# Linear attention in slots: the gates cut behind the scan, and values and scores used one slot later

## The chip, the cores and the metric

The kernel runs on one core of a Trainium2 chip. The core has a matrix engine (TensorE, PE in the profile; its weight loads are listed apart as PEld), a vector engine (VectorE, DVE), a scalar engine (ScalarE, ACT), and a queue that issues transfers (SyncE, SP); a further engine, GpSimd (POOL), does almost nothing here. Matrix products are written to PSUM, which is held in banks; all other tiles lie in SBUF. The metric is the time of one execution on the device in microseconds (us). The times shown are the median and the extremes of three runs; the profile is of one execution more, whose own time stands beside it.

## The reference

One encoder block on a sequence of 1024 positions and 1024 features, in float32. What is computed in the part that the change touches is gated linear attention in two directions, with four heads, keys of 128 and values of 256 features:

```
z   = code @ up + bias                      # per direction, 16 -> 512
lg  = max(log_sigmoid(z) / 16, -0.5)
b   = cumsum(lg)        within a chunk
q'  = q * exp(b);  k' = k * exp(-b)
scores = where(mask, q' k'^T, 0)
o   = scores @ v + q' @ state
state = exp(b_last) * state + k_tail^T v
out = rms_norm(o_fwd + o_bwd) * silu(r)
```

The forward direction takes a position's own key in, the backward direction does not. Around it stand the input projection of the normalised input, a windowed attention with eight heads, the projections of both branches with their sigmoid gates, and a feed-forward block.

## The kernel before

The kernel is one unrolled program. Matrix products are of float32 values split in a high and a low part (`vh` and `vl`, `kth` and `ktl`, `sh` and `sl`, `wh` and `wl` for weights): ACT makes the high part by a copy, VectorE the low part by a subtraction, and `mm3` adds three products. All of them go through `mm`, so they bear the line L76. Products on unsplit float32 tiles (`th` with `q2f`, `thb` with `q2b`, `en` with `q2f` and `q2b`) go through the same line.

The stage of interest runs over four heads (`hd`) and eight chunks of 128 positions each (`c`), so 32 steps n = hd * 8 + c, in a software pipeline of slots. The table `at` says which function runs in which slot for which chunk:

- `g_gates` (L514) in slot n, for two chunks at once, so in even slots alone. It loads `qk`, does the matmul of `lrS` with `upS` (z), the exponential (L537), a minimum (L539), a logarithm (L540), the scan (L544) into `cs`, the chunk sums `sm`, three subtractions into `e` (L550 to L553), two exponentials over `cs` and `e` (L557, L558), and four products: two into `en` and two into `q2` (L560 to L564), of which the first is `q2f` and the second `q2b`. `e` and `cs` have one buffer each.
- `g_scores` (L566) in slot n + 2: it loads and splits the values (`vr`; `vh`, `vl`), transposes `en` on PE (L578) and splits the result (`kth`, `ktl`), makes the scores of both directions (`sc`), merges them with the mask `tri` into `sp` (L587, L588) and splits that (`sh` L591, `sl` L592).
- `g_out` (L594) in slot n + 3: the products of keys and values (`kv`), the running forward state `pf` (L608), its scaled copy `th` (L607), a copy `kb` for the backward state (L610), and the output `o` from `sh`, `sl`, `vh`, `vl`, `th` and `q2f`, copied to `ob` (L619).
- `g_back_out` (L633) in slot `cb`: the backward share from `thb` and `q2b`, then the next step of the backward state (`g_back`), and for even chunks the normalisation of two chunks (L651).
- `g_turn` (L653) in slot `tt`: two transposes on PE, a copy (L659) and two transfers to DRAM scratch. Both chunks of a pair have the same `tt`.

Within a slot the functions run in the order gates, turns, backward output, output, scores, and `slot` spreads `n` filler matmuls between them. Fillers are the matmuls of the dense projections that later stages need (`dense`, `fill`); what is left over is done in the windowed attention behind. The order on PE is the program's own (`manual_schedule`). On the other engines a planner fixes the order when the program is built, by the order in which instructions are written and by when it thinks their inputs are ready; each engine then runs its list in that order.

PSUM tiles of this stage come from `chtile`, a ring of four banks (`ch`); the dense projections use four others (`mm`). SBUF tiles of the stage come from `gtile`, by tag, with two buffers where nothing else is said.

Of the kernel before, what the change touches and what calls it, by code (L numbers as in the profile page):

```python
# [9 lines left out]
FR = mybir.dt.float32r  # L10
# [4 lines left out]
P = 128  # L15
# [3 lines left out]
NH = 4  # L19
NC = 8  # L20
# [10 lines left out]
def body(tc, i, out):  # L31
    nc = tc.nc
    with ExitStack() as root:
# [8 lines left out]
        def nm(s):  # L42
            uid[0] += 1
            return f"{s}_{uid[0]}"
# [4 lines left out]
        def chtile(shape, dt=F32):  # L49
            return psc.tile(list(shape), dt, tag="ch", name=nm("ch"))  # L50
# [24 lines left out]
        def mm(o, a, b, start, stop):  # L75
            nc.tensor.matmul(o, a, b, start=start, stop=stop)  # L76
# [116 lines left out]
        def fill(n):  # L193

            while n > 0 and dense:
                try:
                    next(dense[0])
                    n -= 1
                except StopIteration:
                    dense.pop(0)  # L200

        def need(key):
            while key not in scr:
                fill(12)

        def slot(stages, n):

            stages = [f for f in stages if f] or [lambda: None]
            done = 0
            for j, f in enumerate(stages):  # L210
                f()
                t = n * (j + 1) // len(stages)
                fill(t - done)
                done = t
# [195 lines left out]
        with tc.manual_schedule(engines={mybir.EngineType.PE}):  # L410
# [8 lines left out]
            for k in range(KT):  # L419
# [5 lines left out]
                c = slice((k % 4) * P, (k % 4 + 1) * P)  # L425
# [17 lines left out]
            for f in range(0, NG, 2):  # L443
                x_first(f)
                if f == 0:
                    for s in range(2):
                        v = chtile((P, HT))
# [41 lines left out]
        for s in range(2):  # L489
            c = slice(s * HT, (s + 1) * HT)  # L490
# [18 lines left out]
        def gtile(tag, shape=(P, 256), dt=F32, bufs=2):  # L509
            return gt.tile(list(shape), dt, tag=tag, name=nm(tag), bufs=bufs)  # L510

        gla = {}

        def g_gates(hd, c):  # L514


            pr = Chunk()
            for j in range(2):
                a = gla[hd, c + j] = Chunk()
                a.pr, a.j, a.t = pr, j, slice(j * P, (j + 1) * P)  # L520
            s, co = c // 4, (c % 4) * P
            for nme in ("q", "k"):
                need((f"{nme}{hd}", s))
            qk = gtile("qk", (P, 2, 256))
            nc.sync.dma_start(out=qk[:, 0], in_=scr[f"q{hd}", s][:, co:co + 256])
            nc.sync.dma_start(out=qk[:, 1], in_=scr[f"k{hd}", s][:, co:co + 256])
            if hd == 0:

                r = rstd[:, c * P:(c + 2) * P]
                nc.vector.scalar_tensor_tensor(qk[:, 0], qk[:, 0], 128 ** -0.5, r, op0=ALU.mult, op1=ALU.mult)  # L530
                nc.vector.tensor_tensor(qk[:, 1], qk[:, 1], r, op=ALU.mult)
            z = chtile((P, 2, 256))
            for d in range(2):
                mm(z[:, d], upS[:, d, hd * P:(hd + 1) * P], lrS[:, c * P:(c + 2) * P], True, True)
            e = gtile("e", (P, 2, 2, P), bufs=1)
            ef = e.rearrange("p d j t -> p (d j t)")
            nc.scalar.activation(ef, z.rearrange("p d t -> p (d t)"), AF.Exp, scale=-1.0)  # L537

            nc.vector.tensor_scalar(ef, ef, float(np.expm1(8.0)), None, op0=ALU.min)  # L539
            nc.scalar.activation(ef, ef, AF.Ln, bias=ones[:, 0:1])  # L540

            cs = gtile("cs", (P, 2, 2, P), bufs=1)
            csf = cs.rearrange("p d j t -> p (d j t)")
            nc.vector.tensor_tensor_scan(csf, mask.rearrange("p c t -> p (c t)"), ef, 0.0, op0=ALU.mult, op1=ALU.add)  # L544

            pr.sm = gtile("sm", (P, 2, 2, 2), bufs=16)
            nc.vector.tensor_scalar(pr.sm, cs[:, :, :, 63:128:64], -1.0 / 16, None, op0=ALU.mult)
            nc.vector.tensor_tensor(pr.sm[:, :, :, 1], pr.sm[:, :, :, 1], pr.sm[:, :, :, 0], op=ALU.subtract)

            nc.vector.tensor_tensor(e[:, 0], cs[:, 0], cs[:, 0, :, 63:64].to_broadcast([P, 2, P]), op=ALU.subtract)  # L550
            nc.vector.tensor_tensor(e[:, 1, :, 1:P], cs[:, 1, :, 0:P - 1], cs[:, 1, :, 63:64].to_broadcast([P, 2, P - 1]),
                                    op=ALU.subtract)
            nc.vector.tensor_scalar(e[:, 1, :, 0:1], cs[:, 1, :, 63:64], -1.0, None, op0=ALU.mult)  # L553

            x1 = cs.rearrange("p d j t -> p d (j t)")
            x2 = e.rearrange("p d j t -> p d (j t)")
            nc.scalar.activation(csf, ef, AF.Exp, scale=-1.0 / 16)  # L557
            nc.scalar.activation(ef, ef, AF.Exp, scale=1.0 / 16)  # L558
            pr.en = gtile("en", (P, 2, 256))
            nc.vector.tensor_tensor(pr.en[:, 0], x2[:, 0], qk[:, 1], op=ALU.mult)  # L560
            nc.vector.tensor_tensor(pr.en[:, 1], x1[:, 1], qk[:, 1], op=ALU.mult)
            pr.q2 = (gtile("q2f"), gtile(f"q2b{c}", bufs=(3, 2, 2, 1)[c // 2]))
            nc.vector.tensor_tensor(pr.q2[0], x1[:, 0], qk[:, 0], op=ALU.mult)
            nc.vector.tensor_tensor(pr.q2[1], x2[:, 1], qk[:, 0], op=ALU.mult)  # L564

        def g_scores(hd, c):  # L566

            a = gla[hd, c]
            need((f"v{hd // 2}", c))
            vr = gtile("vr", bufs=1)  # L570
            nc.sync.dma_start(out=vr, in_=scr[f"v{hd // 2}", c][:, (hd % 2) * 256:(hd % 2) * 256 + 256])
            a.vh = gtile("vh", dt=FR)
            a.vl = gtile("vl", dt=FR)
            nc.scalar.activation(a.vh, vr, AF.Copy)
            nc.vector.tensor_tensor(a.vl, vr, a.vh.bitcast(F32), op=ALU.subtract)
            kt = chtile((P, 2, P))
            for d in range(2):
                nc.tensor.transpose(kt[:, d], a.pr.en[:, d, a.t], ident)  # L578
            a.kth = gtile("kth", (P, 2, P), FR)
            a.ktl = gtile("ktl", (P, 2, P), FR)  # L580
            nc.scalar.activation(a.kth, kt, AF.Copy)
            nc.vector.tensor_tensor(a.ktl, kt, a.kth.bitcast(F32), op=ALU.subtract)
            sc = chtile((P, 2, P))
            for d in range(2):
                mm(sc[:, d], a.pr.en[:, d, a.t], a.pr.q2[d][:, a.t], True, True)
            sp = gtile("sp", (P, P))
            nc.scalar.copy(sp, sc[:, 0])  # L587
            nc.vector.copy_predicated(sp, tri, sc[:, 1])  # L588
            a.sh = gtile("sh", (P, P), FR)
            a.sl = gtile("sl", (P, P), FR)  # L590
            nc.vector.tensor_copy(a.sh, sp)  # L591
            nc.vector.tensor_tensor(a.sl, sp, a.sh.bitcast(F32), op=ALU.subtract)  # L592

# [72 lines left out]
        at = {}  # L666
        last = 0
        for n in range(NH * NC):
            hd, c = divmod(n, NC)
            cb = hd * NC + NC + 3 + (NC - 1 - c)  # L670
            tt = cb + c % 2 + 2
            for j, (t, f) in enumerate(((n, g_gates), (n + 2, g_scores), (n + 3, g_out),
                                        (cb, g_back_out), (tt, g_turn))):
                if j or c % 2 == 0:
                    at[t, j + (j == 4 and c % 2)] = (f, hd, c)
                last = max(last, t)
        with tc.manual_schedule(engines={mybir.EngineType.PE}):
            fill(24)
            for t in range(last + 1):
                n = 46 if t < 3 else 20 if t < 6 else 15 if t < NH * NC + 3 else 12 if t < last - 1 else 18  # L680
                slot([(lambda v=at[t, j]: v[0](*v[1:])) if (t, j) in at else None for j in (0, 5, 4, 3, 2, 1)], n)
        glas.close()


# [202 lines left out]
        for n in range(2 * KT):  # L887
            g, t = divmod(n, KT)
# [522 lines left out]
```

## Time and profile before

| | us |
|---|---|
| median of three runs | 1656.65 |
| fastest and slowest run | 1655.84, 1657.62 |
| the profiled execution | 1657.74 |
| its span, first to last instruction | 1656.0 |
| PE busy in the span | 1640.2 |
| VectorE busy in the span | 1238.4 |
| ACT busy in the span | 878.7 |

The profile is a page about the one profiled execution, and a set of views of its trace: the busy time of each engine in a stretch of the span, groups of equal instructions (by line, engine, operation, and tile written <- tiles read), the waits (who stood idle until whose instruction ended), and the single instructions in order of time. Times in it count from the first instruction. Matmuls overlap each other, so the busy time of PE holds no idle time shorter than that overlap. An engine's wait is put down to the instruction that released it last.

### The profile page before, as it was taken

To read this page: it belongs to the slowest core of one execution; us is meant where nothing else is said; L and a number is where in the kernel's file an instruction comes from. 1 tells how busy PE (TensorE), PEld (TensorE's weight loads), DVE (VectorE), ACT (ScalarE), POOL (GpSimd) and SP (SyncE) were. 2 spreads that over 40 slices of the span, in tenths; PEclk is the share of its full clock that TensorE was granted. 3 is DMA by queue.
4 is the path that set the end of the run, shared out by engine and by line. 5 is a ranking of instruction groups with operands and counts; after the bars stand their busy time and mean duration, and the time that the engine had idled before them with its cause. 6 is when DMAs were issued, how large, how long until landed. Compare 5 with 4: busy or idle time off the path is not lost.

```text
span 1656.0 us, 23230 instructions
## 1 busy us (share of the span) xinstructions
PE 1640.2 (99%) x7636; PEld 1357.4 (82%) x7636; DVE 1238.4 (75%) x2548; ACT 878.7 (53%) x1847; POOL 0.2 (0%) x4
## 2 busy tenths in 40 slices
PE   9999999999999999999999999999999999999999
PEld 7888888788888888887888888888888888888887
DVE  8766676677864998756886579887777778779655
ACT  8522234688887587766555456433333333354442
POOL 0000000000000000000000000000000000000000
PEclk9999999999999999999999999999999999999999
DMA  7444336444435633327866645353234443496433
GB/s 234 140 140 146 117 99 194 122 124 137 137 116 162 202 103 108 96 77 251 260 211 188 180 141 162 108 178 109 90 110 152 158 140 134 163 346 197 146 97 120
DMA packets 157497, 252.38 MB, mean 152 GB/s; under 512 B 18142, under 2 KB 43486, under 8 KB 157376
## 3 DMA queue, kind: packets, MB, share of 16 engines
q1 hardware_dynamic: 157376, 250.90, 47.7%
q8 instruction: 60, 0.98, 0.2%
q14 instruction: 61, 0.50, 0.1%
HBM read 183.46 MB, written 67.37 MB: 151 GB/s over the span
## 4 chain that ended last, share of the span: by engine, by line
PE 86%; DVE 6%; ACT 5%; DMA 2%; issue 1%; SPq 0%; DVEq 0%; ACTq 0%
PE mm L76 28%; PE mm L306 9%; PE mm L308 9%; PE mm L307 9%; PE mm L1224 7%; PE ch L76 5%; PE ch L1224 5%; PE ch L308 4%; PE ch L306 4%; PE ch L307 4%; PE ch L847 1%; DVE cs L544 1%; DVE wl L72 1%; DMA kvr<-skv 1%; ACT wh L70 1%
## 5 line engine op out<-in xcount | busy, mean ns | idle before, releaser
L72 DVE TENSOR_TENSOR wl<-wr,wh 128x512 fp32r<-128x512 f32 x226 | 154.2, 685 | 52.0 <-ACT wh L70 48.6
L298 ACT ACTIVATE wh<-ws 128x512 fp32r<-128x512 f32 x132 | 83.3, 632 | 199.2 <-PE mm L307 103.8
L70 ACT ACTIVATE wh<-wr 128x512 fp32r<-128x512 f32 x226 | 140.5, 626 | 86.1 <-PE mm L76 59.1
L76 PE MATMUL mm<-wl,xh 128*128 128x512 f32 x320 | 131.4, 411 | 0.0
L76 PE MATMUL mm<-wh,xh 128*128 128x512 f32 x320 | 130.8, 409 | 0.0
L76 PE MATMUL mm<-wh,xl 128*128 128x512 f32 x320 | 130.5, 408 | 0.0
L299 DVE TENSOR_TENSOR wl<-ws,wh 128x512 fp32r<-128x512 f32 x132 | 90.3, 684 | 28.9 <-ACT wh L298 27.6
L298 ACT ACTIVATE wh<-wr 128x512 fp32r<-128x512 f32 x69 | 43.6, 632 | 123.7 <-issue 49.4
L298 ACT ACTIVATE wh<-a 128x512 fp32r<-128x512 f32 x64 | 40.5, 633 | 89.9 <-PE ch L1224 42.3
L299 DVE TENSOR_TENSOR wl<-a,wh 128x512 fp32r<-128x512 f32 x64 | 44.2, 690 | 41.9 <-ACT wh L298 41.3
L76 PEld LDWEIGHTS mm<-wh,xl 128*128 128x128 f32 x320 | 60.3, 188 | 10.4
L76 PEld LDWEIGHTS mm<-wl,xh 128*128 128x128 f32 x320 | 60.3, 189 | 9.9
L1224 PE MATMUL mm<-hh,wh 128*128 128x512 f32 x176 | 68.5, 389 | 0.0
L1224 PE MATMUL mm<-hl,wh 128*128 128x512 f32 x176 | 68.5, 389 | 0.0
L1224 PE MATMUL mm<-hh,wl 128*128 128x512 f32 x176 | 68.5, 389 | 0.0
L76 PEld LDWEIGHTS mm<-wh,xh 128*128 128x128 f32 x320 | 60.3, 188 | 9.9
L76 PE MATMUL mm<-xl,wh 128*128 128x512 f32 x160 | 65.6, 410 | 0.0
L76 PE MATMUL mm<-xh,wh 128*128 128x512 f32 x160 | 64.7, 405 | 0.1
L76 PE MATMUL mm<-xh,wl 128*128 128x512 f32 x160 | 57.7, 401 | 0.0
L1194 DVE TENSOR_TENSOR hl<-hr,hh 128x512 fp32r<-128x512 f32 x75 | 51.3, 684 | 4.8 <-ACT hh L1193 4.8
L1224 PE MATMUL ch<-hh,wh 128*128 128x512 f32 x132 | 51.3, 389 | 0.0
L1224 PE MATMUL ch<-hl,wh 128*128 128x512 f32 x132 | 51.3, 389 | 0.0
(566 smaller groups left out, 4870.5 us busy)
## 6 DMA issues: line engine op xcount, KB each, us to landing
wr<-in_w_fi_dram SPq DMA_DIRECT2D x102, 256.0 KB, 2.8
wr<-in_w_f_dram SPq DMA_DIRECT2D x80, 256.0 KB, 2.8
wr<-in_w_t_dram SPq DMA_DIRECT2D x80, 256.0 KB, 2.8
B<-c SPq DMA_DIRECT2D x44, 256.0 KB, 2.1
T<-tx SPq DMA_DIRECT2D x44, 256.0 KB, 2.6
a<-in_w_fo_dram SPq DMA_DIRECT2D x44, 256.0 KB, 5.3
hr<-T SPq DMA_DIRECT2D x44, 256.0 KB, 2.7
wr<-in_w_ob_dram SPq DMA_DIRECT2D x32, 256.0 KB, 3.0
```

The costliest lines, as they stand in the source:

```text
L70: nc.scalar.activation(h, raw, AF.Copy)
L72: nc.vector.tensor_tensor(l, raw, h.bitcast(F32), op=ALU.subtract)
L76: nc.tensor.matmul(o, a, b, start=start, stop=stop)
L298: nc.scalar.activation(h, src, AF.Copy)
L299: nc.vector.tensor_tensor(l, src, h.bitcast(F32), op=ALU.subtract)
L306: nc.tensor.matmul(o, h[:, c], x[kk][0], start=start and kk == 0, stop=False, skip_group_check=True)
L307: nc.tensor.matmul(o, h[:, c], x[kk][1], start=False, stop=False, skip_group_check=True)
L308: nc.tensor.matmul(o, l[:, c], x[kk][0], start=False, stop=kk == nk - 1, skip_group_check=True)
L544: nc.vector.tensor_tensor_scan(csf, mask.rearrange("p c t -> p (c t)"), ef, 0.0, op0=ALU.mult, op1=ALU.add)
L847: nc.tensor.transpose(pt[:, h], a.p[:, h, (kb - a.b0) * P:(kb - a.b0 + 1) * P], ident)
L1194: nc.vector.tensor_tensor(l, r, h.bitcast(F32), op=ALU.subtract)
L1224: nc.tensor.matmul(ys[m], a[:, c], b, start=f0, stop=f1, skip_group_check=True)
```

## The change

`g_gates` is cut in two. The first half, which keeps the name, ends behind the scan and the chunk sums `sm`. The second half, `g_powers`, holds the subtractions, the two exponentials and the four products, and runs one slot later, ahead of all else in that slot. `g_out` runs in slot n + 4, and `g_back_out` and `g_turn` one slot later with it, so there are 46 slots where there were 45. The order within a slot becomes gates, powers, turns, backward output, output, scores. `vh`, `vl`, `kth`, `ktl`, `sh`, `sl` and `q2f` get a third buffer, `vr` a second. The numbers of fillers are 46 in slots 0 and 1, 30 in slots 2 and 3, and 15 from there up to slot 35, where they were 46 in slots 0 to 2, 20 in slots 3 to 5, and 15 up to slot 34. No arithmetic is added or taken away.

```diff
+            pr.qk, pr.e, pr.cs = qk, e, cs
             pr.sm = gtile("sm", (P, 2, 2, 2), bufs=16)
...
+        def g_powers(hd, c):
+
+            pr = gla[hd, c].pr
+            qk, e, cs = pr.qk, pr.e, pr.cs
+            ef, csf = (v.rearrange("p d j t -> p (d j t)") for v in (e, cs))
             nc.vector.tensor_tensor(e[:, 0], cs[:, 0], cs[:, 0, :, 63:64].to_broadcast([P, 2, P]), op=ALU.subtract)
...
-            pr.q2 = (gtile("q2f"), gtile(f"q2b{c}", bufs=(3, 2, 2, 1)[c // 2]))
+            pr.q2 = (gtile("q2f", bufs=3), gtile(f"q2b{c}", bufs=(3, 2, 2, 1)[c // 2]))
...
-            vr = gtile("vr", bufs=1)
+            vr = gtile("vr", bufs=2)
...
-            a.vh = gtile("vh", dt=FR)
-            a.vl = gtile("vl", dt=FR)
+            a.vh = gtile("vh", dt=FR, bufs=3)
+            a.vl = gtile("vl", dt=FR, bufs=3)
...
-            a.kth = gtile("kth", (P, 2, P), FR)
-            a.ktl = gtile("ktl", (P, 2, P), FR)
+            a.kth = gtile("kth", (P, 2, P), FR, bufs=3)
+            a.ktl = gtile("ktl", (P, 2, P), FR, bufs=3)
...
-            a.sh = gtile("sh", (P, P), FR)
-            a.sl = gtile("sl", (P, P), FR)
+            a.sh = gtile("sh", (P, P), FR, bufs=3)
+            a.sl = gtile("sl", (P, P), FR, bufs=3)
...
-            cb = hd * NC + NC + 3 + (NC - 1 - c)
+            cb = hd * NC + NC + 4 + (NC - 1 - c)
             tt = cb + c % 2 + 2
-            for j, (t, f) in enumerate(((n, g_gates), (n + 2, g_scores), (n + 3, g_out),
+            for j, (t, f) in enumerate(((n, g_gates), (n + 2, g_scores), (n + 4, g_out),
                                         (cb, g_back_out), (tt, g_turn))):
                 if j or c % 2 == 0:
                     at[t, j + (j == 4 and c % 2)] = (f, hd, c)
                 last = max(last, t)
+            if c % 2 == 0:
+                at[n + 1, 6] = (g_powers, hd, c)
...
-                n = 46 if t < 3 else 20 if t < 6 else 15 if t < NH * NC + 3 else 12 if t < last - 1 else 18
-                slot([(lambda v=at[t, j]: v[0](*v[1:])) if (t, j) in at else None for j in (0, 5, 4, 3, 2, 1)], n)
+                n = 46 if t < 2 else 30 if t < 4 else 15 if t < NH * NC + 4 else 12 if t < last - 1 else 18
+                slot([(lambda v=at[t, j]: v[0](*v[1:])) if (t, j) in at else None for j in (0, 6, 5, 4, 3, 2, 1)], n)
```

## The prediction

> **What bounds the kernel now.** I read the head of the page first, then the busy time of the engines in the linear-attention stage, then the waits of TensorE there, and last the order of single instructions around one such wait. The page says that TensorE is the whole kernel: it is busy for 99% of the span, at the full clock from end to end, so time is won only where TensorE stands still.
>
> ```profile
> span 1656.0 us, 23230 instructions
> ## 1 busy us (share of the span) xinstructions
> PE 1640.2 (99%) x7636; PEld 1357.4 (82%) x7636; DVE 1238.4 (75%) x2548; ACT 878.7 (53%) x1847; POOL 0.2 (0%) x4
> ...
> PEclk9999999999999999999999999999999999999999
> ```
>
> The next view gives busy time by stretch: start and end, length, then PE, PEld, DVE and ACT with their counts, the granted clock, DMA share and GB/s. The first row is the part of the stage in which all its steps run; the second is one of its fullest 20 us.
>
> ```profile
> 280.00:497.00 217.00, 211.39 (x1173) 179.05 (x1172) 162.36 (x484) 173.26 (x489) 0.00 (x0) 1.00 0.42 126
> 460.00:480.00 20.00, 19.46 (x110) 16.42 (x109) 15.62 (x50) 19.43 (x61) 0.00 (x0) 1.00 0.37 115
> ```
>
> PE is idle for 217.00 - 211.39 = 5.6 us of this stretch, a third of its idle time in the whole span (1656.0 - 1640.2 = 15.8 us). ACT, at 173.26 of 217 us (80%) and 19.43 of 20 at its fullest, is the engine next in line. What PE waits for between 250 and 540 us stands in two lists of waits (total us, times, longest), weight loads first, matmuls second; no other release of PE is listed there.
>
> ```profile
> PEld ch L76 <- DVE sh L591: 4.7, 6, 1.2
> PEld ch L76 <- DVE sl L592: 2.1, 7, 0.4
> PEld ch L76 <- ACT th L607: 1.5, 2, 0.7
> PEld ch L76 <- ACT kb L610: 0.8, 2, 0.4
> PEld ch L76 <- DVE ktl L582: 0.6, 1, 0.6
> PEld ch L76 <- ACT kth L581: 0.4, 1, 0.4
> ```
>
> ```profile
> PE ch L76 <- DVE sh L591: 3.4, 4, 1.0
> PE ch L76 <- ACT th L607: 1.1, 2, 0.5
> PE ch L76 <- DVE ktl L582: 0.4, 1, 0.4
> PE ch L76 <- DVE sl L592: 0.2, 1, 0.2
> ```
>
> The names matter: `sh`, `sl`, `kth` and `ktl` are what `g_scores` leaves for `g_out`, one slot later in the program. How one of these waits comes about is seen on VectorE and on PE (start us, length us, instruction, idle before).
>
> ```profile
> 330.05 0.42 DVE L561 TENSOR_TENSOR en<-cs,qk 128x256 f32<-128x256 f32 x1 [0.43 <-ACT cs L557]
> 330.40 0.42 DVE L563 TENSOR_TENSOR q2f<-cs,qk 128x256 f32<-128x256 f32 x1
> 330.73 0.29 DVE L588 COPY_PREDICATED sp<-tri,ch 128x128 f32<-128x128 uint32 x1
> 330.93 0.42 DVE L560 TENSOR_TENSOR en<-e,qk 128x256 f32<-128x256 f32 x1
> 331.27 0.42 DVE L564 TENSOR_TENSOR q2b<-e,qk 128x256 f32<-128x256 f32 x1
> 331.60 0.22 DVE L591 CAST sh<-sp 128x128 fp32r<-128x128 f32 x1
> 331.74 0.47 DVE L608 SCALAR_TENSOR_TENSOR pf<-pf,dec,ch 128x256 f32<-128x256 f32 x1
> 332.13 0.28 DVE L592 TENSOR_TENSOR sl<-sp,sh 128x128 fp32r<-128x128 f32 x1
> ```
>
> ```profile
> 330.52 0.28 PE L76 MATMUL ch<-vl,kth 128*128 128x256 f32 x1
> 330.64 0.28 PE L76 MATMUL ch<-vh,ktl 128*128 128x256 f32 x1
> 331.87 0.39 PE L76 MATMUL ch<-vh,sh 128*128 128x256 f32 x1 [0.96 <-DVE sh L591]
> ```
>
> The four products with the gate powers (`en`, `q2f`, `en`, `q2b`) stand on VectorE's queue around `sp` and ahead of `sh`; nobody needs them for another ten microseconds (below), yet PE stands at `sh`. Matmuls of this shape start 0.12 us apart (330.52 to 330.64); the one on `sh` comes 1.23 us after its forerunner, so 1.11 us are lost there.
>
> **The change, part by part.** Three marks on TensorE's order of work serve the sums below: the gate matmuls of two even slots in a row (`lrS`), a filler matmul ahead of the second, and the first transpose that reads the powers of the first pair.
>
> ```profile
> 362.83 0.41 PE L76 MATMUL ch<-lrS,upS 98*128 98x256 f32 x2
> ...
> 375.51 0.39 PE L76 MATMUL mm<-wh,xl 128*128 128x512 f32 x1
> 375.73 0.41 PE L76 MATMUL ch<-lrS,upS 98*128 98x256 f32 x2
> ...
> 381.14 0.38 PE L578 MATMUL ch<-ident,en 128*128 128x128 f32 x2
> ```
>
> *Values and scores used a slot later.* `g_out` moves from n+3 to n+4, and with it `g_back_out` and `g_turn`; each keeps every instruction, and the two 64 KB transfers of each `g_turn` leave on SP's queue a slot later, with nobody in this stage reading them. `sh`, `sl`, `kth`, `ktl` get a slot more. A slot is 6.45 us (half of 12.90, 362.83 to 375.73), and the longest of these waits is 1.2 us, so all of them should go: 4.7 + 2.1 + 0.6 + 0.4 = 7.8 us. That is the main term.
>
> How much a wait costs PE has to be chosen, since the list of matmuls gives 3.4 + 0.4 + 0.2 = 4.0 us for the same causes. The start times decide: 1.11 us lost at 331.87, where the matmul row counts 0.96 of idle. A matmul's recorded length overlaps the next one, so the idle before it is shortened, and short waits (`sl`, 7 times, against 1 in the matmul list) vanish. I take 7.8 and keep 4.0 for the range. The Trainium skill, "Perfetto Trace Analysis", section "Identifying the Most-Contended Engine", says likewise that the matmul row's occupancy is a poor measure because pipelined matmuls hide what is missing, and that the busy share of the weight loads is better; by its rule the sum is 7.8 us and without it 4.0 us, and the start times agree with it.
>
> *Gates in two halves.* Nothing is added or removed: after the scan and `sm`, three subtractions, two exponentials and four products become `g_powers`, issued first in slot n+1. On VectorE these are 4 x 0.42 us of products by the rows above, and on ACT two exponentials, which stand in the ACT groups (busy us, mean ns, idle before) so:
>
> ```profile
> L557 ACT ACTIVATE cs<-e 128x512 f32<-128x512 f32 x14 | 8.8, 629 | 5.2 <-DVE e L553 4.9
> L558 ACT ACTIVATE e<-e 128x512 f32<-128x512 f32 x14 | 8.7, 624 | 0.0
> ...
> L659 ACT COPY ot<-ch 128x256 f32<-128x256 f32 x22 | 8.0, 365 | 2.3 <-PE ch L657 2.1
> ```
>
> So 1.25 us of ACT and about 2.7 us of VectorE (1.7 of products, estimated 1.0 for the subtractions, two of the same size and one small) leave every even slot for the odd one behind it. Because `cb` moves by one, the two `g_turn` of a pair (2 x 0.365 us of ACT) and the normalisation in `g_back_out` of an even chunk move from even to odd slots too. Before, all four bursts fall in the even slot and none in the odd; after, the even slot keeps exp, min, ln and scan. Nothing is gained on the sum of an engine, but the backlog at the end of an even slot shrinks. The powers become later; they are needed by the transposes of `en` in slot n+2. The last power of the pair marked above, and the next pair's first write of `e`, were here:
>
> ```profile
> 369.67 0.42 DVE L564 TENSOR_TENSOR q2b<-e,qk 128x256 f32<-128x256 f32 x1
> ```
>
> ```profile
> 376.52 0.59 ACT L537 ACTIVATE e<-ch 128x512 f32<-128x512 f32 x1
> ```
>
> The pair whose gate matmul is at 362.83 has its last power at 370.09 and its first transpose at 381.14: 11.05 us of cover. A whole slot of delay (6.45) leaves 4.6 us. The single buffers `e` and `cs` are tighter: the next pair writes `e` at 376.52, 6.43 us after that last read, so a full slot of delay just uses this up. What then waits is ACT's exponential, with one of the four `ch` banks held behind it, and behind it in ACT's order the copies of `ot` and the scan's chain, none of which PE needs at once. In fact the delay should be less than a slot, since `g_powers` is first in its slot and its inputs are ready by then. I cost it at 0, from -0.5 (earlier bank release) to +3 us.
>
> *Buffers.* Third buffers for `vh`, `vl`, `kth`, `ktl`, `sh`, `sl`, `q2f` hold what now lives one slot longer; they cost space only, and without them the added slot would be a wait again. The second `vr` lets SP issue the load of the values before the last split has read the first; SP's queue cannot get later by it. Cost 0.
>
> *Slots and filler.* There are 46 slots for 45. Filler matmuls in the stage: before 24 + 3x46 + 3x20 + 29x15 + 8x12 + 2x18 = 789, after 24 + 2x46 + 2x30 + 32x15 + 8x12 + 2x18 = 788. The rest is done in the attention stage behind as before, so PE's own work is unchanged and the extra slot costs nothing by itself. The slots at the start are shorter, and between the second gate matmul and the transposes that need it lie 30 + 30 + 10 filler matmuls: at the 0.22 us from 375.51 to 375.73 this is an estimated 15 us, more than the 7.3 us from 362.83 to 370.09. Cost 0, up to +1.
>
> *What is late next.* `th` (1.5 us) and `kb` (0.8 us). The running state `pf` still passes from slot to slot, so `th` gets no more time, only a shorter queue ahead of it on ACT. I leave both as they are; if they went too, 2.3 us more.
>
> **Sum.** Against the profiled execution, 1657.74 us (its span 1656.0 and 1.7 around it): 1657.74 - 7.8 = 1649.9. It lies 1.1 above the median of the runs shown, 1656.65, and 1656.65 - 7.8 = 1648.9, which I round to 1649.0. All six rows of weight-load waits gone is 10.1 us: 1646.5; another 0.9 us, half the distance between the slowest and the fastest run (1657.62 and 1655.84), gives the lower end, 1645.6.
>
> **The rivals.**
> *Half the gain.* Only what the matmul list shows is real, or the waits come back as `th` and `kb`, since ACT is at 19.43 of 20 us in places and PE asks for more of it per microsecond once its own gaps are gone: 1656.65 - 4.0 = 1652.7. For it: ACT's load. Against it: the start times, and a stage-wide ACT share of 80%.
>
> *It doesn't do what it says.* The waits are not about one slot but about throughput or about the banks; then a slot more only shifts them: about 1656.7. In this kernel that would be the ring of four `ch` banks, through which every product of the stage goes and which the change leaves at four, while it buys SBUF buffers. Against it: the releasers listed are the tiles `sh` and `sl`, and the only row that names the emptying of a bank, `kb`, is 0.8 us. The Trainium skill, "Perfetto Trace Analysis", section "Optimization Strategy", warns that a gap that repeats on the engine that should be saturated can mean too little SBUF or PSUM for the next tile; by that rule, read for PSUM, nothing is won, and the releasers in this trace do not agree.
>
> *Slower: the powers come too late.* If VectorE and ACT, in odd slots that now also carry turns and normalisation, bring `en` and `q2` more than the 4.6 us beyond one slot, PE stands at the transposes of each even slot. There are 14 of them in the stretch (count of the exponential rows), so each microsecond beyond that point costs 14 us; from 7.8 / 14 = 0.56 us on it eats the gain, and at 1 us the time is 1656.65 - 7.8 + 14 = 1662.9. For it: `e` and `cs` are single, so one late pair delays the next. Against it: VectorE has 162.36 of 217 us, and the powers stand first in their slot.
>
> **How the numbers follow.** The forecast (all or nearly all waits on the four split tiles gone, 1646 to 1651) 0.60; half the gain 0.16; no change 0.11, of which 0.03 by the bank rule; slower 0.13. A difference of 0.2% is 3.3 us, about what a measurement of this kernel tells from none. So faster is 0.60 + 0.16 = 0.76, same 0.11, slower 0.13. The range leaves out the slower case and a little of either end: 1645.6 to 1656.8.
>
> **What would show it.** After: in the list of waits the rows of PEld on `sh`, `sl`, `ktl`, `kth` are gone or under 1 us together, PE's idle time in this stage is under 2.5 us, and the distance of two gate matmuls in the slots that lost a wait falls towards the 12.9 us of 362.83 to 375.73. On VectorE, `sp`, `sh`, `sl` run ahead of `en`. I am wrong if `L578` or the matmuls with `q2f` appear as waiting for `en` or `q2`, if `th` and `kb` grow past 3 us, if the exponential at L537 waits for VectorE and a matmul behind it for its bank, or if the attention stage behind starts later, with its loads waiting for space that the larger pool holds.

## The result, and the profile after

| | before | after |
|---|---|---|
| median (us) | 1656.24 | 1642.09 |
| fastest and slowest run | 1655.44, 1657.62 | 1641.55, 1643.34 |
| the profiled execution | 1657.74 | 1642.39 |
| its span | 1656.0 | 1640.6 |
| up to the first gate matmul (`lrS`) | 256.4 | 255.5 |
| linear attention: to the last transpose of `g_turn` | 275.9 | 264.9 |
| windowed attention and its projection: to the last matmul of `obh` with `wh` | 358.4 | 354.8 |
| the rest | 765.3 | 765.4 |

The medians beside each other are those of the runs on one chip. The changed kernel takes 0.9915 of the time before (95% interval 0.9898 to 0.9932): 14.15 us less. The prediction was 1649.0, a gain of 7.65 us, with 1645.6 as the lower end, so the direction and the stage are right, and the gain is nearly twice the forecast and outside the range. The profiled execution of before (1657.74) is slower than all four of its runs, so about 1 us of the 15.4 us between the two spans is scatter.

The four lower rows of the table are stages of the two traces, cut at three marks on PE: the first matmul of `lrS` (256.4, after 255.5), the last transpose of `ob` (532.3, after 520.4), and the last product of the attention's output (890.7, after 875.2). Two stages became shorter, linear attention by 11.0 us and the windowed attention behind it by 3.6 us. The lead's 0.9 us lies within what this mark shows between kernels that share everything ahead of it (255.3 to 256.7). This is where the last transposes stand in the views by source line, before and then after (the count, shortest, median and longest length in ns, first and last start in us):

```profile
L657 PE MATMUL ch<-ident,ob x64: 270/271/273, 363.5 to 532.3; 128*128 128x128 f32 x64
```

```profile
L663 PE MATMUL ch<-ident,ob x64: 269/272/273, 355.9 to 520.4; 128*128 128x128 f32 x64
```

The head of the page after:

```profile
span 1640.6 us, 23222 instructions
## 1 busy us (share of the span) xinstructions
PE 1632.3 (99%) x7636; PEld 1357.1 (83%) x7636; DVE 1239.0 (76%) x2548; ACT 878.3 (54%) x1847; POOL 0.2 (0%) x4
```

The matmuls are the same 7636, and VectorE and ACT do the same work to within 0.6 us. Yet PE's busy time fell from 1640.2 to 1632.3. Before, the matmul on `sh` at 331.87, which waited, is recorded with 0.39 us, and the one at 339.36, which starts 0.12 us behind its forerunner, with 0.28; recorded lengths also overlap the next start. So busy time holds part of the waiting. The busy time of the weight loads hardly changed (1357.4 and 1357.1). Half of the 15.4 us shows as busy time (7.9) and half as idle time (15.8 to 8.3, so 7.5). The stretch that the prediction looked at, in the view by stretch after (start and end, length, then PE, PEld, DVE and ACT, the granted clock, DMA share, GB/s):

```profile
280.00:491.00 211.00, 211.00 (x1199) 182.34 (x1197) 164.62 (x491) 178.53 (x505) 0.00 (x0) 1.00 0.44 132
```

PE was idle for 5.6 us of this stretch before and is not idle at all now. In the list of waits between 250 and 522 us, PE has no row left, weight loads included: not only `sh`, `sl`, `ktl` and `kth`, but also `th` and `kb`. In the attention stage (523 to 875 us) PE's weight loads still wait (total us, times, longest):

```profile
PEld ch L76 <- DVE pl L859: 2.7, 3, 1.9
PEld mm L76 <- ACT obh L883: 0.9, 1, 0.9
PEld ch L76 <- DVE mx L823: 0.9, 2, 0.6
PEld mm L76 <- DVE obl L884: 0.7, 2, 0.5
...
```

The same list of the kernel before, which the prediction did not use, adds up to 11.9 us against 7.3 here (all rows of either, shown or not):

```profile
PEld ch L76 <- DVE mx L815: 2.2, 5, 0.6
PEld mm L76 <- DVE obl L876: 1.8, 2, 1.2
PEld ch L76 <- ACT kTh L776: 1.8, 1, 1.8
PEld ch L76 <- DVE pl L851: 1.5, 4, 0.6
PEld mm L76 <- ACT obh L875: 1.5, 2, 0.8
...
```

The change touches no line of that stage. Why it became shorter is a question for the experiments.

Why PE no longer stands at `sh` is seen at about the time of the prediction's example (there the seventh chunk, here the ninth), on VectorE and then on PE, after:

```profile
331.64 0.29 DVE L594 COPY_PREDICATED sp<-tri,ch 128x128 f32<-128x128 uint32 x1
331.98 0.42 DVE L567 TENSOR_TENSOR en<-cs,qk 128x256 f32<-128x256 f32 x1
332.33 0.22 DVE L597 CAST sh<-sp 128x128 fp32r<-128x128 f32 x1
332.46 0.42 DVE L569 TENSOR_TENSOR q2f<-cs,qk 128x256 f32<-128x256 f32 x1
332.80 0.28 DVE L598 TENSOR_TENSOR sl<-sp,sh 128x128 fp32r<-128x128 f32 x1
```

```profile
340.00 0.28 PE L76 MATMUL ch<-vh,ktl 128*128 128x256 f32 x1
340.12 0.28 PE L76 MATMUL ch<-vh,sh 128*128 128x256 f32 x1
```

On VectorE one of the powers still stands between `sp` and `sh`, where before there were two, and another between `sh` and `sl`. `sh` is done at 332.55; PE's matmul on it starts 7.6 us later (340.12), 0.12 us after the matmul ahead. Over all 32 chunks the time from the end of `sh` to the first matmul on it is 6.3 to 8.9 us, where before it was 0.1 to 4.1.

### The profile page after: what moved, and what is told of

The parts are those of the page before. It is cut to its first block, busy times and chain, and to the rows that moved or that the text cites. A ratio compares the mean times of both kernels' runs of the same rounds, so it can differ in the third digit from the quotient of the medians.

```text
span 1640.6 us, 23222 instructions
## 1 busy us (share of the span) xinstructions
PE 1632.3 (99%) x7636; PEld 1357.1 (83%) x7636; DVE 1239.0 (76%) x2548; ACT 878.3 (54%) x1847; POOL 0.2 (0%) x4
## 4 chain that ended last, share of the span: by engine, by line
PE 94%; DVE 2%; DMA 2%; ACT 1%; issue 0%; SPq 0%; ACTq 0%; DVEq 0%
PE mm L76 32%; PE mm L306 9%; PE mm L308 9%; PE mm L307 9%; PE ch L76 8%; PE mm L1232 7%; PE ch L1232 5%; PE ch L306 4%; PE ch L308 4%; PE ch L307 4%; PE ch L855 1%; DMA kvr<-skv 1%; DMA lo<-b 0%; PE ch L663 0%; PE ch L584 0%; PE ch L805 0%
## 5 line engine op out<-in xcount | busy, mean ns | idle before, releaser
L1232 PE MATMUL ch<-hh,wl 128*128 128x512 f32 x132 | 51.4, 390 | 0.0
```

What stands on the lines that cost most here:

```text
L1232: nc.tensor.matmul(ys[m], a[:, c], b, start=f0, stop=f1, skip_group_check=True)
```

## The experiments

Each kernel ran with the kernel before beside it on the same chip. The waits are the sums of the weight-load lists of the linear-attention stage and of the attention stage; the lengths are those of the stages by the same marks (us). Fillers are the number of filler matmuls that the slots of linear attention hold; the others are done in the attention stage, so lengths of a stage compare only between kernels with nearly the same number. A filler is about 0.23 us. Rows on `lrS` (0.2 or 0.3 us in three of the kernels) belong to the first gate matmul, where the stage begins, and are left out.

| kernel | fillers | median | ratio to before (interval) | waits, lin. att. | waits, att. | length, lin. att. | length, att. |
|---|---|---|---|---|---|---|---|
| before | 789 | 1656.24 | 1 | 10.1 | 11.9 | 275.9 | 358.4 |
| after | 788 | 1642.09 | 0.9915 (0.9898 to 0.9932) | 0 | 7.3 | 264.9 | 354.8 |
| later_only | 788 | 1643.63 | 0.9920 (0.9906 to 0.9933) | 2.0 | 9.0 | 265.8 | 356.4 |
| split_only | 789 | 1650.10 | 0.9960 (0.9946 to 0.9974) | 4.2 | 9.8 | 269.2 | 356.6 |
| fill_only | 773 | 1654.18 | 0.9991 (0.9982 to 1.0000) | 12.8 | 4.9 | 274.5 | 356.4 |
| tail_only | 801 | 1656.34 | 1.0002 (0.9993 to 1.0011) | 10.1 | 11.9 | 278.1 | 358.0 |
| before_788 | 788 | 1653.39 | 0.9978 (0.9970 to 0.9987) | 10.1 | 6.6 | 275.7 | 354.7 |
| after_789 | 789 | 1646.15 | 0.9936 (0.9924 to 0.9949) | 0 | 11.0 | 264.8 | 357.6 |
| after_773 | 773 | 1642.36 | 0.9912 (0.9899 to 0.9926) | 1.6 | 5.7 | 262.5 | 357.2 |
| later_even | 788 | 1644.48 | 0.9920 (0.9905 to 0.9936) | 3.3 | 8.0 | 266.4 | 355.8 |
| split_788 | 788 | 1646.19 | 0.9940 (0.9926 to 0.9954) | 4.1 | 6.1 | 268.8 | 354.1 |
| after_2bufs | 788 | 1642.46 | 0.9915 (0.9901 to 0.9929) | 0 | 6.1 | 264.8 | 353.8 |
| late_powers | 788 | 1643.42 | 0.9922 (0.9908 to 0.9935) | 1.5 | 7.7 | 265.6 | 355.1 |
| after_780 | 780 | 1643.22 | 0.9921 (0.9908 to 0.9933) | 0.4 | 7.4 | 263.2 | 357.0 |

**The slot more alone.** The gates stay whole; `g_out`, `g_back_out` and `g_turn` a slot later, the buffers and the fillers are those of the change.

```diff
-            for j, (t, f) in enumerate(((n, g_gates), (n + 2, g_scores), (n + 3, g_out),
+            for j, (t, f) in enumerate(((n, g_gates), (n + 2, g_scores), (n + 4, g_out),
...
-            cb = hd * NC + NC + 3 + (NC - 1 - c)
+            cb = hd * NC + NC + 4 + (NC - 1 - c)
```

> The gates stay whole; the output step, backward output and turns run a slot later, with the third buffers and the fillers of the change. Theory 'slack' (the extra slot alone removes the waits on the split tiles): in the linear-attention stage the weight-load waits on sh, sl, ktl, kth fall from 7.8 us to under 1, those on th and kb (2.3 us) stay, and the time falls by 7 to 9 us. Theory 'burst' (the pile of gate work in even slots is the cause, and a slot more only moves the waits): under 3 us are won and th grows. For the attention stage behind: theory 'planner' (any edit ahead gives another order of VectorE and ACT there, and so other waits) expects its weight-load waits to be off the 11.9 us of before by 2 us or more in either direction; theory 'earlier' (they fall because the stage ahead leaves no backlog) expects them lower, near the 7.3 us after the change.

It takes 1643.63 us, all but about 1.5 us of the whole gain. Its linear-attention stage is 265.8 us long, 10.1 less than before; `sh`, `sl`, `kth`, and also `th` and `kb`, are gone from its weight loads:

```profile
PEld mm L76 <- ACT st L186: 1.8, 2, 0.9
PEld ch L76 <- DVE ktl L582: 0.9, 3, 0.5
PEld ch L76 <- ACT ot L659: 0.6, 2, 0.3
PEld ch L657 <- DVE ktl L582: 0.5, 1, 0.5
```

(The row on `st` lies at the border of the stages and is counted with the attention.) That `th` and `kb` would stay, as the prediction had it, is wrong already here.

**The cut alone.** The gates are cut as in the change, with `g_out` in slot n + 3, the buffers and the fillers as before.

```diff
+            if c % 2 == 0:
+                at[n + 1, 6] = (g_powers, hd, c)
```

> The gates are cut in two, the output step stays at n + 3, with the buffers and fillers of before. Theory 'slack': the waits on sh, sl, ktl, kth stay above 5 us of 7.8, time within 3 us of before. Theory 'burst': these waits fall below 2 us, time 6 to 9 us lower, and th and kb go as well since the queue of ACT in even slots is shorter. Attention stage: 'planner' any value, 2 us or more off 11.9; 'earlier' 11.9 lowered in proportion to what the stage ahead wins.

It takes 1650.10 us, 0.9960 of the time before. The cut by itself, to which the prediction gave no gain, makes the linear-attention stage 6.7 us shorter, and takes away 6.2 of the 6.8 us that PE waited for `sh` and `sl`:

```profile
PEld ch L76 <- ACT kth L587: 1.6, 3, 0.7
PEld ch L76 <- ACT th L613: 1.3, 2, 0.7
PEld ch L76 <- DVE ktl L588: 0.5, 3, 0.2
PEld ch L76 <- DVE sh L597: 0.4, 2, 0.2
PEld ch L76 <- issue: 0.2, 1, 0.2
PEld ch L76 <- DVE sl L598: 0.2, 1, 0.2
```

The wait on `th` is nearly the same as before (1.5, now 1.3), that on `kb` is gone, and `kth` costs more than it did (0.4, now 1.6). Each of the two theories expected something that did not come: one no such gain, the other that `th` goes too.

On the seventh chunk, that of the prediction's example, one power stands ahead of `sh` on VectorE behind `sp`, where before two did:

```profile
326.34 0.30 DVE L594 COPY_PREDICATED sp<-tri,ch 128x128 f32<-128x128 uint32 x1
326.54 0.42 DVE L569 TENSOR_TENSOR q2f<-cs,qk 128x256 f32<-128x256 f32 x1
326.88 0.22 DVE L597 CAST sh<-sp 128x128 fp32r<-128x128 f32 x1
```

PE waited longest for `sh` on the third, fifth, seventh and ninth chunk (0.9 to 1.2 us each). There the end of `sh` comes 3.05 to 4.13 us behind the start of the last scores matmul before, and 2.00 to 2.38 us with the cut alone. With the later slot alone it comes 3.4 to 4.0 us behind, as late as before, but PE's use of it moves from 3.1 to 4.2 us behind that matmul to 9.0 to 9.5. So the cut makes `sh` sooner, and the later slot asks for it later.

So either part alone does most of the work: 10.1 and 6.7 us of the stage, and both together 11.0. They are two cures of one trouble, and their gains do not add up.

**The numbers of fillers.** The kernel before with the change's numbers in its own slots; and the kernel before with more of them in its last two slots.

```diff
-                n = 46 if t < 3 else 20 if t < 6 else 15 if t < NH * NC + 3 else 12 if t < last - 1 else 18
+                n = 46 if t < 2 else 30 if t < 4 else 15 if t < NH * NC + 3 else 12 if t < last - 1 else 18
```

> The kernel before with the filler numbers of the change (46 in two slots, 30 in two, then 15). Both theories of the linear-attention stage expect its waits to stay at 8 us or grow, since the slots at the start are shorter: time within 3 us of before. Attention stage: 'planner' 2 us or more off 11.9 us of waits; 'earlier' 11.9 within 1 us.

```diff
-                ... else 12 if t < last - 1 else 18
+                ... else 12 if t < last - 1 else 24
```

> The kernel before with 24 instead of 18 fillers in the last two slots of the linear-attention stage, so 12 matmuls (about 2.7 us of TensorE) are done there and not in the attention stage; all else is as before. The linear-attention waits stay at 10.1 us. 'planner': the waits of the attention stage are 2 us or more off 11.9 and the time moves with them; 'earlier': they stay within 1 us and the time within 1.5 us of before.

The first is 1654.18 us, some 2 us faster at the very edge of its interval, in a mixed way: more waits in linear attention (12.8), fewer behind it (4.9). The second is 1656.34, no different from before, and its waits add up to the same 10.1 and 11.9 us, although the order of instructions on ACT and VectorE in the attention stage is another one than before. That was a miss: I had expected another order there to move the time by 2 us at least.

**One filler.** The change has 788 fillers in its slots where before has 789. The kernel before with one fewer, and the changed kernel with one more, both in the last slot:

```diff
-                ... else 12 if t < last - 1 else 18
+                ... else 12 if t < last - 1 else 18 - (t == last)
```

> The kernel before with one filler fewer in the last slot of the linear-attention stage (788 as after the change, for 789). Theory 'filler count' (the gain behind the linear-attention stage comes from the count alone, since the planner then writes another order for VectorE and ACT in the attention stage, the same one as after the change): the linear-attention waits stay at 10.1 us, the attention waits fall from 11.9 towards 7.3 us, and the time falls by 2 to 5 us, to 1651.5 to 1654.5. Theory 'earlier' (the attention stage gains because the stage ahead of it leaves no backlog): within 1 us of before.

```diff
-                ... else 12 if t < last - 1 else 18
+                ... else 12 if t < last - 1 else 18 + (t == last)
```

> The kernel after the change with one filler more in the last slot (789, as before). 'Filler count': the linear-attention stage stays without waits, the attention stage gets nearly the order of before and its waits of 10 to 12 us, the time is 1644.5 to 1647. 'Earlier': the time stays at 1642 within 1 us.

One matmul of 0.23 us, moved from one stage to the next and taken out of no kernel, is worth 3.3 us in the kernel before (1656.66 beside it, 1653.39) and some 3.6 us in the changed one (10.5 us below the kernel before beside it, against 14.15). It lies in the attention stage: 358.4 and 354.7 us before, 357.6 and 354.8 after. Whether it is worth more in the one kernel than in the other can't be told from these runs. The waits of the kernel before with 788 fillers in that stage:

```profile
PEld ch L76 <- DVE pl L851: 2.1, 2, 1.7
PEld mm L76 <- DVE obl L876: 2.1, 2, 1.5
PEld ch L76 <- DVE mx L815: 0.9, 2, 0.6
PEld mm L76 <- ACT st L186: 0.7, 1, 0.7
...
```

The waits on `kTh` (1.8) and `obh` (1.5) of the kernel before are gone and that on `mx` is down from five times to two. In the changed kernel with 789 fillers the rows on `kTh` and `mx` are back, at the head of the list:

```profile
PEld ch L76 <- ACT kTh L784: 2.6, 1, 2.6
PEld ch L76 <- DVE mx L823: 2.2, 5, 0.6
...
```

So this share of the gain comes neither from the cut nor from the later slot, but from the number of fillers that came with them. The program as built shows what goes with it: all kernels here with 788 fillers have one and the same order of ACT's and VectorE's instructions in the attention stage, instruction for instruction, while before and the cut alone (789) share another one. PE's order there shifts by one filler at the same time, and no run parts these two.

**Cut and 788.** If the two causes are separate, the cut alone with 788 fillers is worth the sum of both.

```diff
-                n = 46 if t < 3 else 20 if t < 6 else 15 if t < NH * NC + 3 else 12 if t < last - 1 else 18
+                n = 46 if t < 3 else 20 if t < 6 else 15 if t < NH * NC + 3 else 12 if t < last - 1 else 18 - (t == last)
```

> Only the gates cut in two (output step at n + 3, buffers of before), with 788 fillers. If filler count and linear-attention waits add up: 1650.1 - 3.3 = 1646.8, within 1 us, with the linear-attention waits near the 4.2 us of the run with the cut alone. If they do not add: 1649 to 1651.

1646.19 us, 3.9 below the cut with 789. The linear-attention stage is as with 789 (268.8 against 269.2), the attention stage 2.5 shorter (354.1 against 356.6). At 788 fillers throughout, the medians then read 1653.39 with neither part, 1646.19 with the cut, 1643.63 with the later slot, 1642.09 with both: 7.2, 9.8 and 11.3 us. They were measured on different chips, where the kernel before had medians from 1656.24 to 1656.66, so these differences hold to about half a microsecond.

**Fillers in the changed kernel.** With the sensitivity known, two other numbers were tried, 773 and 780.

```diff
-                ... else 12 if t < last - 1 else 18
+                ... else (11 if t == last - 2 else 10) if t < last - 1 else 18
```

> The kernel after the change with 15 fillers fewer in the slots behind the last gates (773, the count of the run with only the fillers changed), so that the attention stage gets the order of that run, in which its waits were 4.9 us. 'Filler count': no waits in the linear-attention stage, about 5 us of them in the attention stage, 1639 to 1641.5, below the kernel after the change. 'Earlier': 1642 to 1644, since the filler only moves.

```diff
-                ... else 12 if t < last - 1 else 18
+                ... else 11 if t < last - 1 else 18
```

> The kernel after the change with 780 fillers (one fewer in each of the eight slots behind the last gates). The linear-attention stage has no waits as after the change. The attention stage gets yet another order: 'filler count' expects its waits to differ from the 7.3 us after the change by more than 1 us, in either direction, and the time by as much around 1642; if order does not matter, 1642 within 1 us.

Neither beats the change: 1642.36 and 1643.22 us. With 773 the attention stage has fewer waits (5.7), but with its short slots at the end PE waits for the normalised output instead, ahead of the transposes of `g_turn`:

```profile
PEld ch L663 <- ACT ob L657: 1.6, 2, 1.1
```

With 780 the order on ACT and VectorE is yet another one and the waits in the attention stage add up to those of 788 (7.4 and 7.3): another order does not mean another sum of waits, as with the last slots above. What I had expected of the filler count missed in both: the time with 773, the waits with 780.

**Even slots again.** The later slot moves the turns and the normalisation to the slots that hold no gates. If that, and not the distance between maker and user, took `th` and `kb` away, they should come back when the back output and the turns go a slot further, into even slots.

```diff
-            cb = hd * NC + NC + 4 + (NC - 1 - c)
+            cb = hd * NC + NC + 5 + (NC - 1 - c)
...
-                n = ... else 12 if t < last - 1 else 18
+                n = ... else (11 if t % 3 else 10) if t < last - 1 else 18
```

(from the slot more alone; `q2b` and `ob` get a buffer more for the chunks that live longest)

> As the run with the output step a slot later and whole gates, but backward output and turns another slot later, so that turns and the normalisation fall into even slots again, with the gates, as before the change (47 slots, 788 fillers, third buffers for two of q2b and ob). Theory 'backlog' (th and kb wait because ACT's work piles up in even slots, and the move of turns and normalisation to odd slots is what removed them): the waits on th, thb or kb come back with 1.5 us or more, time 2 us or more above 1643.6. Theory 'slack' (the slot more for g_out removes them): no more than 1 us of such waits, time within 1.5 us of 1643.6.

```profile
PEld ch L76 <- ACT kb L610: 1.9, 3, 1.1
PEld ch L657 <- ACT ob L651: 1.0, 3, 0.5
...
```

`kb` comes back and more than it was (1.9 against 0.8). `th` makes PE wait nowhere, but it comes close: the shortest time from its end to the matmul that reads it is 0.24 us, where it is 2.20 us with the later slot alone. The time is 1644.48, 0.85 us above the later slot alone, which lies within the spread of the runs. So the load of the even slots bears on `kb`, and on `th` without bringing its wait back; what else took that wait away is not shown.

**Two buffers.** The changed kernel with every tile's buffers as before.

```diff
-            a.sh = gtile("sh", (P, P), FR, bufs=3)
-            a.sl = gtile("sl", (P, P), FR, bufs=3)
+            a.sh = gtile("sh", (P, P), FR)
+            a.sl = gtile("sl", (P, P), FR)
```

(and so for `vr`, `vh`, `vl`, `kth`, `ktl` and `q2f`)

> The kernel after the change without the additional buffers (two for vh, vl, kth, ktl, sh, sl and q2f, one for vr). The prediction's view ('needed': without them the added slot is a wait again): waits on kth, ktl, sh, vh of 3 us or more in the linear-attention stage, 1645 or more. The rival ('order suffices': in a slot the output step stands ahead of the scores, so that two buffers are free in time): under 1 us of waits, 1642 within 1 us.

1642.46 us against 1642.09, the same, and no waits in the linear-attention stage. The extra buffers buy nothing here.

**Powers still later.** In the program `g_powers` is moved one more slot, to n + 2, ahead of all else there; the transposes that read `en` stand in that same slot. `e` and `cs` get two buffers.

```diff
-                at[n + 1, 6] = (g_powers, hd, c)
+                at[n + 2, 6] = (g_powers, hd, c)
```

> The kernel after the change with the powers two slots behind the gates and not one (first in slot n + 2, in which the scores read them), with two buffers for e and cs. The prediction's slower rival gives one slot of delay 4.6 us of room; a second slot (6.45 us) goes 1.9 us beyond it, so TensorE should stand at the transposes of en in each even slot, 14 x 1.9 = 26 us, time near 1668, if place in the program is what sets the time of the powers. If the planner fills them in as soon as their inputs are ready and queues are free, the waits stay under 2 us and the time within 2 us of 1642.

1643.42 us, and no wait at the transposes of `en`. The product that ends a pair's powers, on VectorE:

```profile
372.06 0.42 DVE L570 TENSOR_TENSOR q2b<-e,qk 128x256 f32<-128x256 f32 x1
```

```profile
375.81 0.28 PE L76 MATMUL ch<-lrS,upS 98*128 98x256 f32 x1
...
380.07 0.38 PE L584 MATMUL ch<-ident,en 128*128 128x128 f32 x2
```

It ran at 372.06, ahead of PE's first matmul of the slot in which it is written (375.81), and 7.6 us ahead of the transposes (380.07; 372.06 + 0.42 = 372.48). Over all 16 pairs the last product is done at least 6.2 us ahead of its transposes (7.1 us after the change, 9.4 before). So VectorE and ACT run ahead of PE here, the slot in which a step is written does not hold it back to that slot, and the powers are late neither by one slot nor by two.

## Why the prediction was right or wrong

**The main term was right.** "All of them should go" holds: the four rows on `sh`, `sl`, `kth` and `ktl` are gone, though the later slot, to which the prediction gave this, leaves 1.4 us on `ktl` when it stands alone. The choice of the weight-load list over the list of matmuls was right too. All six rows of the weight loads gave 10.1 us, the list of matmuls 5.1 (3.4 + 1.1 + 0.4 + 0.2); the stage became 11.0 us shorter in the traces, and the time by 10.5 (1656.66 to 1646.15, at 789 fillers) and 11.3 (1653.39 to 1642.09, at 788) in the medians. The loads' list is right to about a tenth, the matmuls' one short by half. The rule that the prediction weighed, in the Trainium skill's "Perfetto Trace Analysis", section "Identifying the Most-Contended Engine", is about busy shares; taking it over to lists of waits was the prediction's own step. For busy shares this trace agrees: that of the weight loads rose from 82.0 to 82.7%, as it must when the same work takes 0.9% less time, and that of the matmuls only from 99.0 to 99.5%.

**"What is late next" was wrong**, by 2.3 us. The prediction left `th` and `kb` as they were, because "the running state `pf` still passes from slot to slot, so `th` gets no more time". One of those waits before, on VectorE, ACT and PE:

```profile
419.58 0.47 DVE L608 SCALAR_TENSOR_TENSOR pf<-pf,dec,ch 128x256 f32<-128x256 f32 x1
```

```profile
423.50 0.71 ACT L186 ACTIVATE st<-mm,rstdt 128x512 f32<-128x512 f32 x1
424.07 0.54 ACT L607 ACTIVATE th<-pf,dec 128x256 f32<-128x256 f32 x1
```

```profile
424.66 0.48 PE L76 MATMUL ch<-th,q2f 128*128 128x256 f32 x1 [0.52 <-ACT th L607]
```

The state was there at 420.05, and `th` was made at 424.07, right behind another instruction: 4.0 us lay in ACT's queue, none in the passing of the state. Among what ran there in between are a power's exponential (L558 at 420.52) and the normalisation (L651 at 422.31). The same chunk after:

```profile
410.40 0.47 DVE L614 SCALAR_TENSOR_TENSOR pf<-pf,dec,ch 128x256 f32<-128x256 f32 x1
```

```profile
411.62 0.52 ACT L613 ACTIVATE th<-pf,dec 128x256 f32<-128x256 f32 x1
```

```profile
415.87 0.38 PE L76 MATMUL ch<-th,q2f 128*128 128x256 f32 x1
```

`th` now starts 0.75 us behind its state (410.40 + 0.47 to 411.62) and is done 3.7 us ahead of its use (411.62 + 0.52 to 415.87). The prediction gave the shorter queue a clause and no price. The cut alone leaves the wait on `th` (1.3 us) and takes that on `kb`; the later slot takes both. Which instructions of ACT's queue the later slot moves out of the way of `th` stays open: the turns and the normalisation are at most a part of it, since moving them back to even slots takes the shortest lead of `th` down to 0.24 us but brings no wait.

**"Slots and filler" was wrong**, and it is the larger miss. "PE's own work is unchanged and the extra slot costs nothing by itself" holds for the linear-attention stage. But "the rest is done in the attention stage behind as before" does not: from 789 to 788 fillers the time falls by 3.3 us (without the change) to some 3.6 us (with it), in that stage. The prediction wrote down both numbers and put their difference at nothing. With this term the forecast comes to its lower end, 1649.0 - 3.3 = 1645.7, and with `th` and `kb` to 1643.4, against 1642.09 measured. The remaining 1.3 us is less than the distance between the runs of the changed kernel (1641.55 to 1643.34), and no run assigns it.

**"Gates in two halves", costed at 0,** holds beside the later slot, where the cut adds 1.5 us (1643.63 to 1642.09; the two intervals overlap), and not by itself, where it takes 6.7 us off the stage. The prediction had the reason, fewer bursts at the end of an even slot, and set no price on it. "On VectorE, `sp`, `sh`, `sl` run ahead of `en`" was wrong: they still alternate.

**"Buffers": "without them the added slot would be a wait again"** was wrong. With two buffers the time is the same, and no wait appears in the stage.

**The rivals.** Half the gain did not come: ACT, at 178.53 of 211.00 us in the stretch, keeps up. That the bank ring or throughput is the bound is refuted, by the same row and by the two-buffer kernel; by the rule of "Optimization Strategy" in "Perfetto Trace Analysis" (the Trainium skill) a gap that repeats can mean that memory for the next tile is short, but this gap went with buffers and banks left as they were. In its case against this rival the prediction misread one thing: `kb` is not the only row whose instruction reads a bank, `kth` and `ktl` (0.4 and 0.6 us) do so too. The slower rival, powers too late, did not come: after the change they are still at least 7.1 us early, and written two slots behind at least 6.2, so the 4.6 us of room that the prediction counted from slot lengths were not the limit.

**The signs.** PE's idle time in the stretch went under 2.5 us (to none), and the distance of two gate matmuls fell to 12.9 us or less. The longest before, among slots of 15 fillers, and the same two gates after:

```profile
453.63 0.41 PE L76 MATMUL ch<-lrS,upS 98*128 98x256 f32 x2
467.51 0.41 PE L76 MATMUL ch<-lrS,upS 98*128 98x256 f32 x2
```

```profile
438.24 0.40 PE L76 MATMUL ch<-lrS,upS 98*128 98x256 f32 x2
450.21 0.40 PE L76 MATMUL ch<-lrS,upS 98*128 98x256 f32 x2
```

13.88 us there, 11.97 here; no pair of such slots after the change is further apart than 12.88.

## What to carry to other kernels

Price the waits of a matmul engine by its weight loads and by start times, and look at the queue of the engine that makes the late tile before deciding that a dependency, not that queue, holds it. Moving a consumer a slot later and parting the burst that delays its producer are substitutes here: 9.8 and 7.2 us alone, 11.3 together. Where a planner orders the other engines, a count that differs by a single instruction can move the time by a fifth of a per cent, so a comparison of two versions should hold such counts equal, or measure that one instruction by itself.

## What was not expected

A filler matmul of about 0.23 us changed the time by more than 3 us in either kernel, through waits in a stage that no edit touched. Twelve fillers more changed nothing, and eight or fifteen fewer in the changed kernel made it no faster, so it is not a matter of more or less. Whether the other order on ACT and VectorE or the place of PE's own fillers decides isn't settled.

The busy time of PE on the page fell by 7.9 us with the same 7636 matmuls: about half of the 15.4 us between the two spans had been counted as work.
